# A max-pool kernel: 64 of the first load's windows moved to the last load

## The chip, the cores and the metric

One core of a Trainium2 chip runs the kernel. The metric is the device time in microseconds (us) of one execution. Each run on record also has its span, which begins with the profiler's first record and is some 1.75 us shorter; a profile shows one such execution, whose own time is on record too. A ratio between two kernels below is the mean time of one kernel's runs over that of the other's in the same rounds, so it is not quite the ratio of the medians that are quoted.

A *row* below is one partition's piece of a transfer. A transfer over 128 partitions gives each of the 16 DMA engines 8 rows and one tiny completion packet (the small store has 144 packets, 128 + 16).

## The reference

The input is 32 x 256 rows of 4096 float32, 134.2 MB. Each row is cut into 256 windows of 16, and the result is the maximum of each window, 8.4 MB.

```python
for i in range(output_size):                      # 256
    start = int(i * length / output_size)
    end = int((i + 1) * length / output_size)     # 16 elements
    result[:, :, i] = np.max(x[:, :, start:end], axis=-1)
```

## The kernel before

The 2,097,152 windows are spread over 128 partitions, 16384 to each. They are read in 17 loads, all issued by SyncE: a short one of FIRST windows, 15 of 1024 windows (64 KB per partition), and a last one with what remains. VectorE takes the maxima (a full load in two reduces, 872 and 152 windows, so that the larger part of the buffer comes free early) into the tile `kept`. There are three stores: two big ones from `kept` on SyncE's queue (q1 in the profile, behind the loads), and the small one with the last load's result on ScalarE's queue (q10).

```python
CHUNK = 1024
GAP = 152
FIRST = 132
LOADS_A, LOADS_B = 9, 6
last = total - FIRST - (LOADS_A + LOADS_B) * CHUNK     # 892
# ...
            if n == FIRST:
                nc.sync.dma_start(
                    out=ring[:, CHUNK * W : (CHUNK + n) * W], in_=xn
                )
                pooled(dst, CHUNK, n)
            else:
                low = n_loads % 2 * (CHUNK + GAP)      # two halves of the ring
                moved = n_loads // 2 % 2
                at = low + moved * GAP
                nc.sync.dma_start(out=ring[:, at * W : (at + n) * W], in_=xn)
                if n == CHUNK:
                    # two reduces, 872 and 152 windows
                    # ...
                else:
                    end = (at + CHUNK) * W
                    last_kept = ring[:, end - n : end]
                    pooled(last_kept, at, n)           # the last reduce
# ...
nc.scalar.dma_start(out=og[:, full : full + last], in_=last_kept)   # small store, q10
tc.no_sync_barrier()
for dst, src in stores:
    nc.sync.dma_start(out=dst, in_=src)                             # big stores, q1
```

Of the kernel before, what the change touches and what calls it, by code (L numbers as in the profile page):

```python
# [1 line left out]

# [4 lines left out]


@with_exitstack
def kernel(  # L10
    ctx: ExitStack,
    tc: tile.TileContext,
    x: bass.AP,
    output_size: bass.AP,
    out: bass.AP,
):








    nc = tc.nc
    P = nc.NUM_PARTITIONS
    fp32 = mybir.dt.float32

    B, C, L = x.shape
    O = int(output_size)  # L30
    assert L % O == 0, (L, O)
    W = L // O
    total = B * C * O // P
    assert B * C * O % P == 0

    CHUNK = 1024
    GAP = 152
    FIRST = 132
    LOADS_A, LOADS_B = 9, 6
    last = total - FIRST - (LOADS_A + LOADS_B) * CHUNK  # L40
    assert 0 < last and last * (W + 1) <= CHUNK * W

    pool = ctx.enter_context(tc.tile_pool(name="pool", bufs=1))
    ring = pool.tile([P, 2 * (CHUNK + GAP) * W], fp32, tag="ring", name="ring")
    kept = pool.tile([P, total - last], fp32, tag="kept", name="kept")

    xw = x.flatten_outer_dims().rearrange("r (o w) -> (r o) w", w=W)
    ow = out.flatten_outer_dims().rearrange("r o -> (r o)")

    def pooled(dst, at, n):  # L50

        nc.vector.reduce_max(  # L52
            out=dst,
            in_=ring[:, at * W : (at + n) * W].rearrange("p (n w) -> p n w", w=W),
            axis=mybir.AxisListType.X,
        )

    taken = 0

    def group(n):  # L60

        nonlocal taken
        span = slice(taken * P, (taken + n) * P)
        taken += n
        return (
            xw[span].rearrange("(p n) w -> p (n w)", p=P),
            ow[span].rearrange("(p n) -> p n", p=P),
        )

    stores = []  # L70
    n_loads = 0
    base = 0
    for g, loads in enumerate(
        ([FIRST] + [CHUNK] * LOADS_A, [CHUNK] * LOADS_B + [last])
    ):
        xg, og = group(sum(loads))
        a = 0
        for n in loads:
            xn = xg[:, a * W : (a + n) * W]
            dst = kept[:, base + a : base + a + n] if n != last else None  # L80
# [8 lines that stand above are left out]
                low = n_loads % 2 * (CHUNK + GAP)  # L89
# [4 lines that stand above are left out]
                    cut = CHUNK - GAP if moved else GAP  # L94
                    parts = [(0, cut), (cut, n)]
                    for u, v in parts if moved else parts[::-1]:
                        pooled(dst[:, u:v], at + u, v - u)
# [3 lines that stand above are left out]
                    pooled(last_kept, at, n)  # L101
                n_loads += 1
            a += n
        full = a - last if g else a
        stores.append((og[:, 0:full], kept[:, base : base + full]))
        base += full
    assert taken == total

    nc.scalar.dma_start(out=og[:, full : full + last], in_=last_kept)
    tc.no_sync_barrier()  # L110
    for dst, src in stores:
        nc.sync.dma_start(out=dst, in_=src)


# [1 line left out]
_INS = ['x', 'output_size']  # L116
_OUTS = [((32, 256, 256), 'float32')]

_NUMBERS = {'output_size': 256}


# [26 lines left out]
```

## Time and profile before

| What | Before |
|---|---|
| device time, median (6 runs; the prediction had three, 335.11) | 334.96 us (334.92 to 335.2) |
| share of the span in which the DMA engines are taken | 98.7% (q1) + 0.3% (q10) |
| VectorE busy | 83% |
| one full load: transfer / its reduces | 19.34 us / 17.28 us |
| first load issued, landed | 0.73, 5.8 us |
| last reduce begins, small store issued | 313.27, 328.32 us |

The lines of VectorE's timeline (start, length, what, idle time before it and what ended it) show the start, which the change touches:

```profile
5.86 2.35 DVE L52 TENSOR_REDUCE kept<-ring 128x132 f32<-128x2112 f32 x1 [5.86 <-DMA ring<-in_x_dram]
25.17 17.28 DVE L52 TENSOR_REDUCE kept<-ring 128x872 f32<-128x13952 f32 x2 [16.96 <-DMA ring<-in_x_dram]
```

After the first reduce VectorE idles for 17 us until the first full load is there.

### The profile page before, as it was taken

The numbers are of one execution on the slowest core, as the hardware profiler recorded it, in microseconds if no ns is written. First come the engines' busy times: TensorE is split into PE (matmuls) and PEld (weight loads), VectorE is DVE, ScalarE is ACT, GpSimd is POOL, SyncE is SP. The second block draws the span as 40 slices with busy tenths as digits, with TensorE's granted clock in tenths as the row PEclk, the third lists the DMA queues.
The fourth block names the chain that finished last, engine by engine and source line by source line (L and its number), as shares of the span: only waits on it lengthen the run. The fifth ranks groups of instructions, "written<-read, shape, count | busy, mean of one in ns | idle before, by whom it ended". The sixth has DMA issues, their size and how long they took to land.

```text
span 333.4 us, 113 instructions
## 1 busy us (share of the span) xinstructions
DVE 276.5 (83%) x32; POOL 0.2 (0%) x4
## 2 busy tenths in 40 slices
DVE  2009979797997979799797979979797997979993
POOL 0000000000000000000000000000000000000000
DMA  9898989999898989999898989999898989899997
GB/s 381 377 503 377 495 385 480 401 401 480 377 503 377 503 377 480 401 393 488 377 503 377 503 377 480 401 425 456 377 503 377 503 377 495 385 455 438 397 402 317
DMA packets 2880, 142.61 MB, mean 428 GB/s; under 512 B 320, under 2 KB 320, under 8 KB 448
## 3 DMA queue, kind: packets, MB, share of 16 engines
q1 hardware_dynamic: 2736, 142.15, 98.7%
q10 hardware_dynamic: 144, 0.46, 0.3%
HBM read 134.22 MB, written 8.39 MB: 428 GB/s over the span
## 4 chain that ended last, share of the span: by engine, by line
DMA 58%; DVE 36%; DVEq 5%; issue 0%; SPq 0%
DMA ring<-in_x_dram 58%; DVE kept L52 36%; DVEq L143 5%; SPq L83 0%
## 5 line engine op out<-in xcount | busy, mean ns | idle before, releaser
L52 DVE TENSOR_REDUCE kept<-ring 128x872 f32<-128x13952 f32 (+2 forms) x31 | 261.5, 8477 | 51.8 <-DMA ring<-in_x_dram 51.8
L52 DVE TENSOR_REDUCE ring<-ring 128x892 f32<-128x14272 f32 x1 | 15.0, 15009 | 0.0
L129 POOL MEMSET const-bfloat16-1.0<- 128x1 bf16 x1 | 0.1, 102 | 0.0
L129 POOL MEMSET const-uint8-127<- 128x1 uint8 x1 | 0.1, 102 | 0.0
L129 POOL MEMSET const-float32-1.0<- 128x1 f32 x1 | 0.1, 99 | 0.0
L129 POOL MEMSET const-float32-0.0<- 128x1 f32 x1 | 0.1, 98 | 0.2 <-issue 0.2
## 6 DMA issues: line engine op xcount, KB each, us to landing
ring<-in_x_dram SPq DMA_DIRECT2D x1, 7136.0 KB, 21.5
out_dram<-kept SPq DMA_DIRECT2D x1, 4674.0 KB, 32.2
out_dram<-kept SPq DMA_DIRECT2D x1, 3072.0 KB, 18.0
ring<-in_x_dram SPq DMA_DIRECT2D x1, 1056.0 KB, 5.1
out_dram<-ring ACTq DMA_DIRECT2D x1, 446.0 KB, 4.2
ring<-in_x_dram SPq DMA_DIRECT2D x15, 24.0
```

The lines of the kernel that those rows point to most:

```text
L52: nc.vector.reduce_max(out=dst, in_=ring[:, at * W : (at + n) * W].rearrange("p (n w) -> p n w", w=W), axis=mybir.AxisListType.X,)
L129: nc = _bacc.Bacc("TRN2", target_bir_lowering=False, num_devices=1)
L143: with _tile.TileContext(nc) as tc:
```

## The change

Its intent is to have data for VectorE sooner: the first load shrinks from 132 to 68 windows per partition (8.25 to 4.25 KB), so that it and all full loads land earlier. The 64 windows go to the last load, 892 to 956, and with it to the last reduce and the small store.

```diff
-    FIRST = 132
+    FIRST = 68
```

## The prediction

> **What bounds the kernel now.** I read the page first, for the bound; then the windows, for the DMA share by stage; then the timeline of VectorE with its idle times; then the DMA issues and the waits of the queue that issues the transfers, for the end; and last the DMA packets in narrow windows of the last microseconds.
>
> From the page:
>
> ```profile
> span 333.4 us, 113 instructions
> ...
> DVE 276.5 (83%) x32; POOL 0.2 (0%) x4
> ...
> q1 hardware_dynamic: 2736, 142.15, 98.7%
> q10 hardware_dynamic: 144, 0.46, 0.3%
> HBM read 134.22 MB, written 8.39 MB: 428 GB/s over the span
> ```
>
> The 16 DMA engines are taken for 98.7% + 0.3% of the span, VectorE for 83%. From the windows (columns: window, its length, VectorE busy, GpSimd busy, clock, DMA share, GB/s):
>
> ```profile
> 20.00:300.00 280.00, 245.83 (x29) 0.00 (x0) 1.00 1.00 433
> 314.00:330.00 16.00, 14.28 (x1) 0.00 (x0) 1.00 0.98 421
> ```
>
> In the middle the DMA share is 1.00 at 433 GB/s, and it is still 0.98 in the tail, where the inputs are all in and results are stored. At 433 GB/s, 142.61 MB need 329.3 us; the other 4 us of the span are the start and the end. The chain of waits of the page seems to say something else (DMA 58%, VectorE 36%), because it follows each load to the reduce that freed its buffer. The timeline shows that this reduce has slack (start, length, what, idle time before it):
>
> ```profile
> 276.74 17.28 DVE L52 TENSOR_REDUCE kept<-ring 128x872 f32<-128x13952 f32 x2 [2.08 <-DMA ring<-in_x_dram]
> ...
> 296.08 17.28 DVE L52 TENSOR_REDUCE kept<-ring 128x872 f32<-128x13952 f32 x2 [2.06 <-DMA ring<-in_x_dram]
> 313.27 15.01 DVE L52 TENSOR_REDUCE ring<-ring 128x892 f32<-128x14272 f32 x1
> 328.32 0.37 ACTq L109 DMA_DIRECT2D out_dram<-ring  x1
> ```
>
> A full load of 1024 windows takes 19.34 us (start to start of its reduces, 296.08 - 276.74), its reduces 17.28 us, so VectorE waits some 2.07 us for each. Only the last reduce has no idle time before it: VectorE was the later one there. The DMA issues say by how much (size, us from issue to landing):
>
> ```profile
> ring<-in_x_dram SPq DMA_DIRECT2D x1, 7136.0 KB, 21.5
> ...
> out_dram<-ring ACTq DMA_DIRECT2D x1, 446.0 KB, 4.2
> ```
>
> The last load was issued at 291.45 (timeline), so it landed near 291.45 + 21.5 = 312.95; its reduce began 0.32 us later. Its result goes out at 328.32 on ScalarE's queue and lands 4.2 us later, at about 332.5. The waits of SyncE's queue confirm that it is what lands last:
>
> ```profile
> SPq L143 <- DMA out_dram<-kept: 17.7, 1, 17.7
> SPq L143 <- DMA out_dram<-ring: 1.0, 1, 1.0
> ```
>
> So it looks as if the end hung on the last reduce. The packets decide whether it really does. Three windows, 329.30 to 329.95, then 329.95 to 330.31, then 330.31 to 330.87 (queue: packets that begin there, MB, share):
>
> ```profile
> q1 hardware_dynamic: 16, 0.39, 141.2%
> ```
> ```profile
> DMA packets 0, 0.00 MB, mean 0 GB/s; under 512 B 0, under 2 KB 0, under 8 KB 0
> ```
> ```profile
> q10 hardware_dynamic: 49, 0.17, 77.5%
> q1 hardware_dynamic: 16, 0.00, 1.6%
> ```
>
> A packet is counted where it begins, so a share can exceed 100%. In the first window each of the 16 engines starts its last row of the big stores (16 x 24.6 KB = 0.39 MB; a row of this size takes 141.2% x 0.65 us = 0.92 us). In the second nothing begins, because these rows are still moving. In the third, the 16 tiny completion packets of q1 and the first rows of the last store (q10) begin together. So the small store, though issued at 328.32, does not move until each engine has finished the big stores, 2.0 to 2.5 us after its issue. The engines are not idle at the handover: **the sum of DMA work sets the end, and the last reduce is only just hidden.**
>
> **What the Trainium skill says.** (1) "DMA: Bandwidth & Descriptors", section "Bandwidth", gives a fabric ceiling of 435.2 GB/s; the 433 GB/s of the middle agrees. (2) The same page, "Issuing engines are not separate DMA queues": transfers of different issuers share the same 16 engines. The trace agrees: q10 begins where q1 ends. The page's round robin by packet, in "Queues, rings and completion order", would let the small rows slip in between; no q10 packet begins before 330.31, so here they wait (or were not ready earlier; the trace can't tell). (3) The same page, "Latency and other measured facts", has about 0.6 us to the first byte on this path. Here the first load is issued at 0.73 and no packet begins before 1.74: 1.0 us. I use the 1.0 us. (4) "VectorE: DVE Perf Modes", section "The perf-mode tier table", says that a reduce has the 1x mode only, which at its 0.96 GHz would be 1.04 ns an element, 16.67 ns a window of 16. The rows by shape agree:
>
> ```profile
> L52 DVE TENSOR_REDUCE kept<-ring 128x872 f32<-128x13952 f32 x15 | 220.3, 14686 | 46.0 <-DMA ring<-in_x_dram 46.0
> L52 DVE TENSOR_REDUCE kept<-ring 128x152 f32<-128x2432 f32 x15 | 40.1, 2676 | 0.0
> ```
>
> (14686 - 2676) / 720 windows = 16.68 ns.
>
> **The change, part by part.** FIRST goes from 132 to 68 windows per partition, the last load from 892 to 956 (16384 - 68 - 15 x 1024). 64 windows x 64 B x 128 partitions = 0.524 MB move from the first load to the last. No instruction or transfer is added or removed, and each engine's order is the same.
>
> - *Start.* The 0.524 MB are 1.21 us at 433 GB/s. The first load and all 15 full loads land 1.21 us earlier, and with them their reduces (from 132 to 68 windows the first one is 1.07 us shorter, in idle time). A load is issued when the larger reduce of two loads before ends; that too comes 1.21 us earlier, and the transfer queue still has the previous load, with 4.6 us to go, in it. Worth nothing by itself: no byte less is moved.
> - *The last load* starts 1.21 us earlier and takes 1.21 us longer: lands at about 312.95 as before. Input bytes are the same.
> - *The last reduce.* VectorE is free 1.21 us earlier, at 313.27 - 1.21 = 312.06, so it now waits 0.9 us for the load and begins near 312.97, 0.30 earlier. It has 64 windows more: 64 x 16.68 ns = 1.07 us, so 15.01 becomes 16.08. It ends at 329.05 instead of 328.28, **0.77 us later**.
> - *The last store* is issued at about 329.09, also 0.77 later, with 478 KB instead of 446. The big stores shrink by the same 32 KB, 0.08 us at 433 GB/s: the sum of the stores stays.
> - *Does the 0.77 us reach the end?* The engines finish the big stores between 330.31 and 330.87 now, and 0.08 earlier then: 330.23 to 330.79. The store issued at 329.09 can begin, by the 1.0 us of the first load, at 330.1. That is before any engine is free. So the wait behind the big stores shrinks from 2.0 to about 1.2 us on the first engine, and absorbs the 0.77. Sum: 0.
>
> The bound on the other side: I know that the small store is ready within 2.0 us of its issue, since on the first engine it began then. If it needs all of this, it begins at 331.1 on every engine. Eight rows with their completion took the first engine some 1.1 us (330.32 to 331.45) and will take 7% more, 1.2 us: 332.3, against the 332.0 at which the last engine finishes now, so +0.3 us.
>
> **The rivals.**
> (a) *The last reduce becomes the bound in full*: +0.77 us, and 0.08 for the longer store: 335.96. For it: the store of the last result lands last, with no idle time on VectorE before it. Against it: the packets of the handover, which leave no gap.
> (b) *The shorter start pays*: 1.21 us less, 333.9. For it: everything to the 15th full load is earlier. Against it: the last load is longer by the same bytes on queues that are full; a gain would need a gap at the start, and none is made or closed.
> (c) *Ready late*: the store needs between 1.2 and 2.0 us from issue to first packet (a store reads another memory than the first load did): 0 to +0.3 us.
> (d) *Transfers run at another rate*, as the rows of each partition lie at other addresses. The rows stay one contiguous piece per partition of tens of KB, so I expect less than 0.1%.
>
> **Range and chances.** I give (sum of 0) 55%, (c) 30%, (a) 10%, (b) or (d) 5%: 0.30 x 0.15 + 0.10 x 0.85 - 0.02 = about +0.1 us on 335.11, so 335.2. The three runs of before spread over 0.26 us; with (a) on one side and that spread on the other I take 334.7 to 335.9. Two per cent are 6.7 us, several times what any rival moves: within 2% is 0.99.
>
> **What would show it right or wrong.** Right: the last reduce takes 16.08 us, begins after about 0.9 us of idle time at 312.97 and ends near 329.05; the last store's time from issue to landing falls from 4.2 to about 3.5 us; q10's first packets begin at about 330.2 to 330.8, at the end of q1's; the first full load's reduce begins at 23.96 instead of 25.17. Wrong: q10's packets begin clearly after q1's completions, with empty DMA windows between (rivals a, c); the last load lands at another time than 312.95 (b, d); full loads take other than 19.34 us.

## The result, and the profile after

The changed kernel took 335.22 us in the median (6 runs, 335.04 to 335.39) against 334.96; the ratio is 1.0006, with a 95% interval of 0.9993 to 1.0019: the same. In a second session it took 334.96 (5 runs) against 335.02, ratio 1.0000. If there is a difference, it is smaller than what the runs of one kernel differ by, some 0.3 to 0.6 us.

The bound is unchanged, from the page of the changed kernel:

```profile
DVE 276.6 (83%) x32; POOL 0.2 (0%) x4
...
q1 hardware_dynamic: 2736, 142.12, 98.7%
q10 hardware_dynamic: 144, 0.49, 0.5%
```

What did move is in VectorE's timeline:

```profile
4.77 1.29 DVE L52 TENSOR_REDUCE kept<-ring 128x68 f32<-128x1088 f32 x1 [4.77 <-DMA ring<-in_x_dram]
24.09 17.28 DVE L52 TENSOR_REDUCE kept<-ring 128x872 f32<-128x13952 f32 x2 [18.03 <-DMA ring<-in_x_dram]
...
295.04 17.28 DVE L52 TENSOR_REDUCE kept<-ring 128x872 f32<-128x13952 f32 x2 [2.08 <-DMA ring<-in_x_dram]
313.19 16.09 DVE L52 TENSOR_REDUCE ring<-ring 128x956 f32<-128x15296 f32 x1 [0.87 <-DMA ring<-in_x_dram]
329.30 0.37 ACTq L109 DMA_DIRECT2D out_dram<-ring  x1
```

All full loads come about 1.05 us earlier (25.17 to 24.09, 296.08 to 295.04). At the last load this is gone: its reduce begins at 313.19, where it began at 313.27, and now waits 0.87 us for the load. It is 1.08 us longer, so the small store is issued 0.98 us later, at 329.30 instead of 328.32. The DMA issues show where this second is lost again (size, us from issue to landing):

```profile
ring<-in_x_dram SPq DMA_DIRECT2D x1, 7648.0 KB, 22.7
...
out_dram<-ring ACTq DMA_DIRECT2D x1, 478.0 KB, 3.3
```

The last load takes 22.7 instead of 21.5 us from issue to landing: what the start won. The small store takes 3.3 instead of 4.2: what the last reduce lost. It spends less time behind the big stores. The waits of SyncE's queue say that it is still last by about the same: 1.1 us after the big stores, where it was 1.0.

```profile
SPq L143 <- DMA out_dram<-kept: 18.8, 1, 18.8
SPq L143 <- DMA out_dram<-ring: 1.1, 1, 1.1
```

The handover of the engines from q1 to q10 takes longer in this profile, though. These are the packets that begin between 330.20 and 332.30 us (queue: packets, MB, time they took as a share of 16 engines), first before, then after:

```profile
q10 hardware_dynamic: 144, 0.46, 55.2%
q1 hardware_dynamic: 16, 0.00, 0.4%
```
```profile
q10 hardware_dynamic: 144, 0.49, 72.8%
q1 hardware_dynamic: 16, 0.00, 0.4%
```

The small store's packets took 55.2% x 2.1 us = 1.16 us per engine before and 72.8% x 2.1 us = 1.53 us after, for 7% more bytes. The rest lies in the first rows. In the window 330.31 to 330.87 before had 49 packets of q10 (shown in the prediction); after has

```profile
q10 hardware_dynamic: 15, 0.06, 65.6%
```

which is 0.656 x 0.56 us x 16 / 15 = 0.39 us a packet; a full row needs about 0.15 in the later windows. So the store reaches the engines just as they come free, and its first row on an engine takes longer. Whether this costs time is asked below.

### The profile page after: what moved, and what is told of

Read it like the earlier page. It is cut to its first block, busy times and chain, and to the rows that moved or that the text cites. A ratio compares the mean times of both kernels' runs of the same rounds, so it can differ in the third digit from the quotient of the medians.

```text
span 333.5 us, 113 instructions
## 1 busy us (share of the span) xinstructions
DVE 276.6 (83%) x32; POOL 0.2 (0%) x4
## 4 chain that ended last, share of the span: by engine, by line
DMA 62%; DVE 36%; SPq 0%; issue 0%; DVEq 0%
DMA ring<-in_x_dram 62%; DVE kept L52 31%; DVE ring L52 5%; SPq L92 0%; SPq L83 0%; DVEq L52 0%
## 5 line engine op out<-in xcount | busy, mean ns | idle before, releaser
L52 DVE TENSOR_REDUCE ring<-ring 128x956 f32<-128x15296 f32 x1 | 16.1, 16086 | 0.9 <-DMA ring<-in_x_dram 0.9
## 6 DMA issues: line engine op xcount, KB each, us to landing
ring<-in_x_dram SPq DMA_DIRECT2D x1, 7648.0 KB, 22.7
```

The lines of the kernel that those rows point to most:

```text
L52: nc.vector.reduce_max(out=dst, in_=ring[:, at * W : (at + n) * W].rearrange("p (n w) -> p n w", w=W), axis=mybir.AxisListType.X,)
```

## The experiments

Two theories. **A**: the sum of DMA work sets the end; the small store has slack behind the big stores, and of a delay of the last reduce only tenths of a us come through. **B**: the last reduce is the bound; its delay of about 1 us passes to the end, and the equal times are a trade of this against the shorter start.

### The changed kernel again

No edit.

> The changed kernel itself, a second time. Theory A (the sum of DMA work sets the end; of the last reduce's delay only some tenths of a us come through): 335.2 us, 0.1 to 0.3 over the kernel before on the same chip. Theory B (the last reduce is the bound, and its delay of about 1 us was made up for by chance or by the shorter start): 335.2 too; this run is to show whether the first full load's reduce again begins at about 24.09 instead of the 23.96 predicted, and the last load again lands near 313.09 instead of 312.95. If the start itself costs this 0.13 us, it does so again; if it was chance, it doesn't.

It took 334.96 us (5 runs, 334.85 to 335.46; before 335.02 on the same chip, 9 runs). The first full load's reduce began at 23.65, not 24.09, and the last reduce at 312.71, not 313.19:

```profile
23.65 17.28 DVE L52 TENSOR_REDUCE kept<-ring 128x872 f32<-128x13952 f32 x2 [18.02 <-DMA ring<-in_x_dram]
...
312.71 16.09 DVE L52 TENSOR_REDUCE ring<-ring 128x956 f32<-128x15296 f32 x1 [0.87 <-DMA ring<-in_x_dram]
```

So what the start cost in the first profile was chance. The time at which the first full load is there differs by 0.4 us between profiles of one kernel, and this stays until the end: both lines above are earlier by 0.44 and 0.48 us. Most experiments below share their start with one of the two kernels, so there are more profiles of it. The six with a first load of 68 windows begin this reduce at 23.65 to 24.09 (mean 23.89), the three with 132 at 24.87 to 25.17 (mean 24.99): 1.10 us earlier, where the bytes say 1.21. The difference of 0.11 is within the scatter. The first packet begins 1.68 to 1.76 us after the span's start in all ten profiles, so the scatter arises after it.

### The last reduce cut, the transfers kept

```diff
-                    pooled(last_kept, at, n)
+                    pooled(last_kept[:, 0:892], at, 892)     # first kernel
+                    pooled(last_kept[:, 0:478], at, 478)     # second kernel
```

(Against the changed kernel.) Both give a wrong result in the windows that are not reduced; the same bytes are loaded and stored.

> The changed kernel with its last reduce over 892 windows instead of 956, so 1.07 us shorter; loads and stores as they were, 64 windows of the result wrong on purpose. Theory A: only what the handover loses comes back, 0.15 to 0.35 us: 334.9 to 335.1. The last store's rows all take some 0.15 us again, none 0.6. Theory B: 1.07 us less, 334.15.

> The changed kernel with its last reduce over half of its windows, 7.97 us shorter; loads and stores as they were, half of the last load's result wrong on purpose. The last store is then ready while the big stores still run. Theory A: no more than with 892 windows, 334.8 to 335.1, although the last reduce ends 8 us earlier. Theory B: at least 2 us less.

They took 335.02 us (5 runs) and 335.07 us (4 runs); before took 335.02 on the same chip, the changed kernel 334.96. The intervals of the ratios to before are 0.9989 to 1.0017 and 0.9988 to 1.0015. Neither taking 1.07 us nor 7.97 us off the last reduce gains anything, and B, which asked for 334.15 and less, is out. The timeline of the second one shows how early its store was issued:

```profile
313.14 8.12 DVE L52 TENSOR_REDUCE ring<-ring 128x478 f32<-128x7648 f32 x1 [0.86 <-DMA ring<-in_x_dram]
321.29 0.37 ACTq L109 DMA_DIRECT2D out_dram<-ring  x1
```

It was issued 8 us earlier than in the changed kernel, and the end did not move: its 478 KB now take their time among the big stores, which end later for it. Between 321.30 and 330.00, then between 330.00 and 332.20, packets of both queues begin:

```profile
q1 hardware_dynamic: 144, 3.35, 90.0%
q10 hardware_dynamic: 73, 0.28, 7.9%
```
```profile
q1 hardware_dynamic: 32, 0.39, 42.2%
q10 hardware_dynamic: 71, 0.21, 24.0%
```

After 330.00 q1 still starts 16 full rows (0.39 MB), where the changed kernel has only the 16 completion packets of q1 left (0.4%). So what q10 takes before 330, q1 takes after it: the order changes, and not the end.

The handover is quicker with a shorter reduce. With 892 windows (the row of 3824 bytes is the changed kernel's) the packets of the store that begin from 330.20 to 332.30 (143 of 144) are

```profile
q10 hardware_dynamic: 143, 0.49, 58.0%
```

which is 1.22 us per engine, against 1.53 in the changed kernel's first profile and 1.25 in its second (59.6%). The slow handover, up to 0.3 us per engine, shows in two profiles that issue the small store less than 1 us before the engines come free: at 329.30 here, and at 329.37 in the kernel with 64 more windows below (64.5%, 1.35 us, against 1.16 in the kernel before). It doesn't show where the store is issued at 328.82 (the changed kernel's second profile) or before.

The times of the profiled executions tell whether it costs anything. From each, take off the time at which the first full load's reduce began, which scatters by chance. The changed kernel leaves 335.28 - 24.09 = 311.19 and 334.85 - 23.65 = 311.20; the one with 892 windows 335.02 - 23.85 = 311.17; the one with 478 windows 335.24 - 24.04 = 311.20. These agree within 0.03 us, with small stores issued between 321.29 and 329.30. The scatter among these four is thus that of the start, and neither the longer reduce nor the slow handover adds to it. The kernel before leaves 335.14 - 25.17 = 309.97, which is 1.22 less: the 1.21 us of bytes that the change moves behind this point.

### The shorter first load alone

```diff
-    FIRST = 132
-    last = total - FIRST - (LOADS_A + LOADS_B) * CHUNK
+    FIRST = 68
+    last = total - 64 - FIRST - (LOADS_A + LOADS_B) * CHUNK
```

(against the kernel before; and the size of `kept` to match). 64 windows per partition are neither loaded nor stored, so the result is wrong.

> One half of the change alone: the first load shrinks to 68 windows and the last stays at 892; the 64 windows in between are neither loaded nor stored (wrong on purpose). 0.524 MB less to load and 0.033 MB less to store, 1.29 us at 433 GB/s. Theory A: 1.2 to 1.4 us less than the changed kernel, 333.9: all that the shorter first load wins is what the longer last load gives back. Theory B: the last reduce begins at about 312.2 and takes 15.01, so ends 2.1 us earlier than in the changed kernel: 333.1.

It took 334.01 us (4 runs), 1.01 under before's median; the ratio is 0.9968 (0.9954 to 0.9981), so the means differ by 1.07. Against the changed kernel's two medians it is 0.95 to 1.21 us less. A's 333.9 is close, B's 333.1 is not, though its last reduce began at 311.83, 1.4 us before the changed kernel's in its first profile, and was 1.08 shorter on top. The shorter first load is worth its bytes; the longer last load gives the same bytes back. It is a little less than the 1.29 us expected, by no more than the runs differ.

### The last reduce delayed, in the kernel before

```diff
+                    pooled(last_kept[:, 0:64], at, 64)       # or 192 and 192
                     pooled(last_kept, at, n)
```

An extra reduce of 64 or 192 windows, overwritten by the full one, delays the small store alone; the results are right.

> The kernel before with one more reduce of 64 windows (1.21 us by the rows of 68 and 152 windows) ahead of its last one; results right, transfers untouched. This is the delay of the last reduce that the change makes, and somewhat more, without its load sizes. Theory A (the DMA sum sets the end, the last store has some 1 us of slack): the store is issued near 329.5, the engines stay busy with the big stores until 330.3 to 330.9, and 0.1 to 0.5 us come through: 335.1 to 335.5. Theory B (the last reduce is the bound): 1.2 us more, 336.2.

> The kernel before with one more reduce of 192 windows (3.34 us) ahead of its last one. Theory A: here the slack is used up; the store is issued near 331.7, begins 0.9 us later on idle engines, and the end comes 3.34 less about 1.1 of slack, 2.0 to 2.5 us later: 337.0 to 337.5, with empty DMA windows of more than 1 us ahead of the last store. Theory B: 3.3 us more, 338.3. No effect at all would say that neither holds.

| Kernel | small store issued | issue to landing | median us | added to 334.97 |
|---|---|---|---|---|
| before | 328.32 | 4.2 | 334.97 (9 runs) | |
| + 64 windows | 329.37 | 3.1 | 335.14 (5 runs) | 0.17 |
| + 192 windows | 331.50 | 2.5 | 336.64 (4 runs) | 1.67 |

The extra reduces delay the store by 1.25 and 3.39 us (the reduces of the last load take 16.26 and 18.40 us together, against 15.01); the issue times in the table lie 1.05 and 3.18 apart, because these two profiles had an earlier start by chance (24.93 and 24.87 against 25.17). With 64 windows 0.17 us comes through, no more than the runs' scatter (ratio 1.0005, 0.9992 to 1.0017). With 192, 1.67 us come through (ratio 1.0051, 1.0035 to 1.0066, so 1.2 to 2.2 us). With the start taken off as above, 0.24 us (310.21 against 309.97) and 1.81 us (311.78) come through in the profiled executions. So of the 3.39 us some 1.6 to 1.7 are absorbed. B asked for 3.3. The direction was A's but my 337.0 to 337.5 missed: I had put the slack at 1.1, from the engine that comes free first. From issue to landing the store needs 2.5 us when nothing is ahead of it and took 4.2 before: 1.7 us of slack on the whole, as the time shows. The packets of the 192 kernel, from 331.50 to 332.33 and from 332.33 to 332.60, show idle engines and then the store's start:

```profile
DMA packets 0, 0.00 MB, mean 0 GB/s; under 512 B 0, under 2 KB 0, under 8 KB 0
...
out_dram<-ring ACTq DMA_DIRECT2D x1, 446.0 KB, 2.5
```
```profile
q10 hardware_dynamic: 26, 0.09, 87.1%
```

The store is issued at 331.50 and no packet begins for 0.83 us. Here alone the last reduce is the bound.

### Half of the change

```diff
-    FIRST = 132
+    FIRST = 100
```

> A first load of 100 windows, last one of 924: half of the change. VectorE and the last load then come to the last reduce at about the same time (312.66 and 312.95). Theory A: 335.0, the same as both within 0.2 us. Theory B: the best of the three, some 0.3 us under the kernel before at most, 334.7 (its last reduce ends 0.2 later than before's, so B would rather say 335.2).

(Against the kernel before.) It took 335.01 us (5 runs) against 334.97, ratio 1.0003 (0.9990 to 1.0015). Its last reduce waits only 0.31 us for the load. The balance of VectorE and the last load, which one might tune by FIRST, is worth nothing that can be measured here.

### The last reduce and its store in two pieces

```diff
-                    pooled(last_kept, at, n)
+                    pooled(last_kept[:, 0:764], at, 764)
+                    pooled(last_kept[:, 764:n], at + 764, n - 764)
-    nc.scalar.dma_start(out=og[:, full : full + last], in_=last_kept)
+    nc.scalar.dma_start(out=og[:, full : full + 764], in_=last_kept[:, 0:764])
+    nc.scalar.dma_start(
+        out=og[:, full + 764 : full + last], in_=last_kept[:, 764:last]
+    )
```

> The changed kernel with its last reduce in two pieces of 764 and 192 windows, each stored as soon as it is done; one more reduce (0.15 us) and one more store. Four fifths of the last result can move 3.3 us earlier, among the big stores. Theory A: the engines' work is the same, so 0 to 0.2 us less than the changed kernel: 334.9 to 335.2. Theory B: the last piece to move is 0.7 us shorter, so 334.5.

(Against the changed kernel.) It took 335.14 us (5 runs, 335.06 to 335.54) against the 334.97 of the kernel before, ratio 1.0007 (0.9995 to 1.0020). B's 334.5 is missed, and A's hope for a tenth is not fulfilled either: the 382 KB of the first piece were issued at 326.00 and landed 6.3 us later. No packet of q10 begins before 329.60, so they too waited behind the big stores. With the start taken off, its profiled execution leaves 335.35 - 23.96 = 311.39 us, 0.2 more than the changed kernel's, so the second store may cost a little; one profile does not show it for sure. The two pieces as the DMA issues have them:

```profile
out_dram<-ring ACTq DMA_DIRECT2D x1, 382.0 KB, 6.3
out_dram<-ring ACTq DMA_DIRECT2D x1, 96.0 KB, 3.4
```

Nothing points to a version that beats both kernels: with the engines taken for 99% of the span, what is left to win is at the very start and after the last byte, and neither the size of the first load nor the split of the small store reaches it.

## Why the prediction was right

It said 335.2 us in a range of 334.7 to 335.9, and the same within 2% at 0.99; 335.22 and 334.96 were measured. That the first of these is so near 335.2 is luck: the sum stood on a base of 335.11 from three runs, which six put at 334.96, and the first profile of the changed kernel had the latest start of the six (24.09).

- *The bound* was named rightly, and the cut reduces show it: 8 us off the last reduce gain nothing.
- *The start, 1.21 us earlier*: 1.10 in the mean of the profiles. Worth its bytes and no more, as the run with the shorter first load alone shows.
- *The last load lands as before*, near 312.95: it was issued at 290.39 and took 22.7, so 313.09 in the first profile; in the second its reduce began 0.48 us earlier. The error is chance of the start, 0.4 us between profiles, which I had not foreseen.
- *The last reduce*: 16.08 us predicted, 16.09 measured; 0.9 us of idle time predicted, 0.87 measured; the small store at 329.09 predicted, 329.30 and 328.82 measured.
- *The absorption*: 3.5 us from issue to landing predicted, 3.3 and 3.4 measured. That the 0.77 is absorbed holds. The term that was mis-sized is the slack. I took it from the first byte on the engine that comes free first (1.0 us after issue, so about 1.0 to spare); the delayed reduces put it at 1.6 to 1.7 us. The engine that comes free last says the same: it does so near 330.87, 2.55 us after the issue at 328.32, and on idle engines the store begins 0.88 us after its issue. In the other direction, the store that arrives just in time has slow first rows, up to 0.3 us per engine, which my sum left out; the profiled executions show that they did not reach the end.
- *The reduce's rate*: the 16.67 ns a window are an estimate from two sections of "VectorE: DVE Perf Modes", the 1x mode of the tier table and the 0.96 GHz of "Specifications"; the rows by shape gave 16.68.
- *The rivals*: (a), 335.96, falls by the cut and by the delayed reduces; (b), 333.9, is what the shorter first load would give alone. Both effects are real, but one is hidden and the other repaid. (c), 1.2 to 2.0 us from issue to first packet, falls by the 0.88 us on idle engines, which also says that the store of the kernel before was ready near 329.2 and waited. (d), another rate, falls by the full loads: 19.36 us (295.04 - 275.68) against 19.34.

The 0.26 us between the first session's medians are no effect of the change that these runs can show: the second session has none, and in the profiled executions the two kernels differ, after the start's scatter is taken off, by the bytes moved and by 0.01 us more. What stays open is why the start scatters by 0.4 us, and why the first rows of a store that arrives just in time are slow.

## What to carry to other kernels

Where the transfers fill the span, as here, moving bytes from the first transfer to the last moves landings and waits around, but not the end; ask of a proposal how many bytes it takes away, or which gap on the DMA engines it closes. A chain of waits that ends in a compute step does not make that step the bound: look whether the transfer that follows it had to queue, and measure the slack by delaying and by shortening the step. Here a step that seemed last could end 8 us earlier for nothing, and about 1.2 us later almost for nothing, while 3.4 us later cost 1.7. Where single runs scatter, find the stage that scatters and take it off: here that left 0.03 us.

## What the Trainium skill lacked or had wrong

- "DMA: Bandwidth & Descriptors", section "Queues, rings and completion order", describes round robin between queues by packet. It does hold, packet for packet of the trace: in the kernel whose last reduce has 478 windows, 74 packets of q1 and 72 of q10 begin between 324.88 and 330.00. But the page does not say how late it sets in under load. That store was issued at 321.29, and until 324.87 only q1's packets begin (70 of them); by the trace its first row begins at 324.88, 3.6 us after the issue. In the split kernel it is 3.6 us too, or slightly more (326.00 to after 329.60); on idle engines it is 0.88 us (331.50 to 332.38). Rows that the engines have already taken in would explain it; no run shows that this is the reason.
- The same page, section "Latency and other measured facts", has about 0.6 us to the first byte. It does not say from where this is counted. From the start of the issuing instruction it was 1.0 us for the first load (0.73 to 1.74) and 0.88 us for a store on idle engines; from the end of that instruction, which takes 0.38 and 0.37 us, it was 0.63 and 0.51 us, so the page is not shown to be wrong.
- No page has the slow first row of a small store that arrives just as the engines come free: 0.39 us a packet in the window of 330.31 to 330.87 instead of 0.15. It did not lengthen the run.
- No page has the chance in the start: the first full load of one and the same kernel is reduced from 23.65 to 24.09 us after the span's start, and the difference lasts to the end: the times of the four profiled executions with the same transfers follow it within 0.03 us.
